# The first image pair of a 3x3 convolution loaded by eight DMAs of sixteen rows instead of one of 128

## The chip, the core and the metric

One core of a Trainium2 chip. The metric is the time of one execution on the device in microseconds (us). The kernel before takes 123.04 us (median of 3 runs, 122.94 to 123.07).

A core has engines with a program each: TensorE (PE in the profile, its weight loads PEld), VectorE (DVE), ScalarE (ACT), GpSimd (POOL) and SyncE (SP), which here only issues transfers. They meet by semaphores. Data moves between the device memory and SBUF (128 partitions, one row of a tile in each) by sixteen DMA engines, which all transfers share. A DMA adds 16 to its semaphore when it has landed.

## The reference

A 3x3 convolution with zero padding of 1 over 16 images of 64 channels and 64 x 64 pixels, 64 output channels, and the addition of a residual, all float32 at the border of the kernel:

```python
batch, c_in, h, w, c_out, k = 16, 64, 64, 64, 64, 3
x_pad = np.pad(x, ((0, 0), (0, 0), (pad, pad), (pad, pad)), mode='constant')
...
output[b, co] += weight[co, ci, kh, kw] * x_pad[b, ci, kh:kh+h, kw:kw+w]
...
return (output + residual).astype(np.float32)
```

x, residual and the output are 16.8 MB each.

## The kernel before

Images go in pairs: two images of 64 channels are 128 rows of 64 x 64 x 4 bytes = 16 KB, one row in each partition. `xr` holds three such pairs, `ro` the whole residual, which becomes the output in place.

```python
x_bc = x.rearrange("b c h w -> (b c) (h w)")
ro = pool.tile([128, NPAIR, NPIX], FP32)
xr = [nc.alloc_sbuf_tensor(f"xr{i}", [128, NPIX], FP32) for i in range(NXR)]   # NXR = 3
...
def load_x(p):
    return nc.sync.dma_start(out=xr[p % NXR][:, :], in_=x_bc[128 * p : 128 * p + 128, :]).then_inc(s_x[p % NXR], 16)
...
def store(pairs):
    return nc.sync.dma_start(out=out_bc[:, pairs, :], in_=ro[:, pairs, :])
```

All transfers are issued by SyncE, in this order. `to_the_front` takes the DMA just emitted and puts it into the program's first block, ahead of the barrier at which the engines meet when the program starts; so the first pair is asked for before anything else happens.

```python
for p in range(NPAIR):                                  # NPAIR = 8
    if p >= NXR:
        nc.sync.wait_ge(s_half, 2 * (p - NXR) + 3)      # ScalarE has read the buffer
    if p == 0:
        to_the_front(load_x(p))
        nc.sync.dma_start(out=wraw[:, :], in_=w_rows[:, :]).then_inc(s_w, 16)
    else:
        load_x(p)
    if p in (0, 1, 3, 5, 7):
        load_ro((p + 1) // 2)
for k in range(NEARLY):                                 # NEARLY = 3, two pairs each
    nc.sync.wait_ge(s_add, 4 * k + 5)
    store(slice(2 * k, 2 * k + 2)).then_inc(s_out, 16)
# ... and at the end of the program
for p in range(2 * NEARLY, NPAIR):
    store(slice(p, p + 1))
```

GpSimd makes the identity and the zero borders. TensorE transposes the weights (through `ps`), VectorE and ScalarE cast them into `wl`. Then for each image ScalarE casts the pair's rows to bfloat16 (`xp`), TensorE does 24 matmuls into one of two halves of PSUM, and VectorE adds the result to `ro`:

```python
for n in range(B):                                      # ScalarE, B = 16
    p, im = divmod(n, 2)
    ...
    if im == 0:
        nc.scalar.wait_ge(s_x[p % NXR], 16 * (p // NXR + 1))
    i = nc.scalar.copy(out=t[64:128, 0:J, :], in_=x4[hp, :, 0, :])
    i.then_inc(s_half, 1)
    ...
    nc.scalar.copy(out=t[0:64, 1 : J + 1, :], in_=x4[hp, :, 1, :]).then_inc(s_pack, 1)
```

Of the kernel before, what the change touches and what calls it, by code (L numbers as in the profile page):

```python
# [15 lines left out]
def kernel(  # L16
# [7 lines left out]
    nc = tc.nc  # L24
# [11 lines left out]
    NXR = 3  # L36
    NXP = 4
    NZERO = 4 + 2 * NXP
    NEARLY = 3
    RES = (slice(0, 1), slice(1, 2), slice(2, 4), slice(4, 6), slice(6, 8))  # L40

# [2 lines left out]
    x_bc = x.rearrange("b c h w -> (b c) (h w)")  # L44
# [7 lines left out]
    xr = [nc.alloc_sbuf_tensor(f"xr{i}", [128, NPIX], FP32) for i in range(NXR)]  # L52
# [8 lines left out]
    s_x = [sem(f"s_x{i}") for i in range(NXR)]  # L61
# [8 lines left out]

    def load_x(p):
        return nc.sync.dma_start(out=xr[p % NXR][:, :], in_=x_bc[128 * p : 128 * p + 128, :]).then_inc(s_x[p % NXR], 16)

    def load_ro(i):
        if i >= 2:
            nc.sync.wait_ge(s_r[i % 2], 16 * (i // 2))
        nc.sync.dma_start(out=ro[:, RES[i], :], in_=res_bc[:, RES[i], :]).then_inc(s_r[i % 2], 16)

    def store(pairs):
        return nc.sync.dma_start(out=out_bc[:, pairs, :], in_=ro[:, pairs, :])  # L80
# [21 lines left out]
    def to_the_front(dma):  # L102

        def fixed(ap):
            t = ap.bass_ap.tensor.name
            return mybir.PhysicalAccessPattern(
                ap=ap.ap, offset=ap.bass_ap.offset, dtype=ap.dtype, memref=t, memsetref=t + "_set", bass_ap=ap.bass_ap
            )  # L110

        front = nc.main_func.blocks[0].instructions
        here = nc.cur_bb.bb.instructions
        ins = here.pop()
        assert ins.name == dma.ins.name
        at = next(
            i for i, e in enumerate(front) if e.engine == ins.engine and isinstance(e, mybir.InstDrain)
        )
        front.insert(at, copy.replace(ins, ins=[fixed(a) for a in ins.ins], outs=[fixed(a) for a in ins.outs]))
# [5 lines left out]
    def weight_block(h, half, d, par, kh):  # L125

        at = 64 * half + 32 * h
        return dict(out=wl[at : at + 32, d, :, par, :], in_=tp[0:32, kh, 0:384].rearrange("p (kw co h) -> p kw co h", kw=3, h=2)[:, :, :, h])

    with tc.tile_critical(no_gpsimd_drain=True):  # L130

        for p in range(NPAIR):
            if p >= NXR:

                nc.sync.wait_ge(s_half, 2 * (p - NXR) + 3)
            if p == 0:
                to_the_front(load_x(p))
                nc.sync.dma_start(out=wraw[:, :], in_=w_rows[:, :]).then_inc(s_w, 16)
            else:
                load_x(p)  # L140
            if p in (0, 1, 3, 5, 7):
                load_ro((p + 1) // 2)
        for k in range(NEARLY):
            nc.sync.wait_ge(s_add, 4 * k + 5)
# [6 lines left out]
            out=ident[:, :],  # L151
            in_=ident[:, :],
# [14 lines left out]
        for n in range(B):  # L167
            p, im = divmod(n, 2)
            hp = slice(64 * im, 64 * im + 64)
            x4 = xr[p % NXR].rearrange("q (j two w) -> q j two w", two=2, w=W)  # L170
            t = xp[n % NXP]
            if im == 0:
                nc.scalar.wait_ge(s_x[p % NXR], 16 * (p // NXR + 1))
            i = nc.scalar.copy(out=t[64:128, 0:J, :], in_=x4[hp, :, 0, :])  # L174
            i.then_inc(s_half, 1)
            if n >= NXP:
                i._wait_ge(s_conv, n - NXP + 1)
            nc.scalar.copy(out=t[0:64, 1 : J + 1, :], in_=x4[hp, :, 1, :]).then_inc(s_pack, 1)  # L178
            if n == 0:
                nc.scalar.wait_ge(s_id, NZERO + 1)  # L180
                for b in blocks[4:]:
                    for h in range(2):
                        i = nc.scalar.copy(**weight_block(h, *b))  # L183
                i.then_inc(s_id, 1)


        nc.vector.wait_ge(s_id, NZERO + 1)
        for k, b in enumerate(blocks[:4]):
# [5 lines left out]
        for n in range(B):  # L194
            p, im = divmod(n, 2)
# [6 lines left out]
            for par in range(2):  # L202
                i = nc.vector.tensor_tensor(  # L203
                    out=o4[hp, :, par, :], in0=psj[64 * par : 64 * par + 64, :, :], in1=o4[hp, :, par, :], op=ADD
# [6 lines left out]

        nc.tensor.wait_ge(s_id, NZERO)
        nc.tensor.wait_ge(s_w, 16)
        wraw3 = wraw.rearrange("p (ci t) -> p ci t", t=9)
        for t in range(9):
            i = nc.tensor.transpose(  # L216
                out=tp[0:32, t // 3, 128 * (t % 3) : 128 * (t % 3) + 128], in_=wraw3[:, :, t], identity=ident[:, :]
            )
        i.then_inc(s_id, 1)
        nc.tensor.wait_ge(s_id, NZERO + 3)  # L220
        with nc.Fori(0, B // NXP, 1, engines=[PE]):
# [18 lines left out]

    for p in range(2 * NEARLY, NPAIR):
        store(slice(p, p + 1))
    with tc.tile_critical(sync_engine=mybir.EngineType.Pool, no_gpsimd_drain=True):
        nc.gpsimd.wait_ge(s_out, 16 * NEARLY)
        tc.free_semaphores([s_w, *s_x, *s_r, s_out, s_id, s_half, s_pack, s_bank, s_conv, s_add])
# [30 lines left out]
```

## Time and profile before

A profile is one execution taken by the hardware profiler; times in it are microseconds from the start of its span.

| | value |
|---|---|
| time, median of 3 | 123.04 us |
| span in the profile | 120.8 us |
| bytes moved | 50.48 MB: 33.70 read, 16.78 written |
| mean rate over the span | 418 GB/s |
| one image pair (2048 KB), median time from issue to landing | 15.3 us |
| ScalarE's first cast of the first pair starts | 7.79 us |
| first convolution matmul starts | 13.78 us |

How to read it: the page gives the busy share of each engine, a strip of forty slices of the span with a digit for tenths of busy time, the share of the DMA queue, the chain of work that ended last, and groups of instructions. Windows give the same for any stretch of the span, and the timeline lists instructions in order. The trace also has a record of each DMA packet (its start, its time and its bytes); a packet here is one row of 16 KB, or a row of the weights of 1152 bytes, or a completion write of 4 bytes at the end of a DMA on an engine. An engine that is idle costs nothing as long as it isn't the one that the others wait for.

### The profile page before, as it was taken

What the parts mean: (1) busy time and instruction counts of PE and PEld (TensorE: products, weight loads), DVE (VectorE), ACT (ScalarE), POOL (GpSimd) and SP (SyncE); (2) the same over time, 40 slices, a digit from 0 to 9 for tenths busy, and PEclk for the clock granted to TensorE, in tenths of its full rate; (3) what the DMA queues carried; (4) which work ended last, traced back from release to release, by engine and by line L of the source; (5) the groups of instructions that cost most, each with busy time, mean ns of one, the idle gap of its engine ahead of it and who ended that gap; (6) DMA issues with size and microseconds to landing.
All of it is one profiled execution on the core that took longest, in us unless ns stands there. A gap on an engine that the chain in (4) does not pass through costs nothing.

```text
span 120.8 us, 734 instructions
## 1 busy us (share of the span) xinstructions
PE 87.9 (73%) x393; PEld 10.7 (9%) x105; DVE 76.0 (63%) x40; ACT 63.1 (52%) x37; POOL 2.4 (2%) x16
## 2 busy tenths in 40 slices
PE   0024499999999999999999999999999990000000
PEld 0011001101010011011111111011111100000000
DVE  0005400789898988989879898988989879500000
ACT  4049959948999923999960999883000000000000
POOL 5200000000000000000000000000000000000000
PEclk9999999999999999999999999999999999855555
DMA  7999999999999999999999999999999999999994
GB/s 168 428 428 428 428 428 434 428 434 434 428 434 434 434 428 434 434 434 434 434 434 423 423 428 434 423 412 434 434 434 434 423 434 434 434 428 434 434 434 174
DMA packets 3504, 50.48 MB, mean 418 GB/s; under 512 B 304, under 2 KB 432, under 8 KB 432
## 3 DMA queue, kind: packets, MB, share of 16 engines
q1 hardware_dynamic: 3504, 50.48, 98.5%
HBM read 33.70 MB, written 16.78 MB: 418 GB/s over the span
## 4 chain that ended last, share of the span: by engine, by line
PE 71%; DVEq 2%; DVE 2%; issue 0%
PE ps L87 53%; PE ps L86 18%; DVEq L130 2%; DVE ro L203 2%
## 5 line engine op out<-in xcount | busy, mean ns | idle before, releaser
L203 DVE TENSOR_TENSOR ro<-ps,ro 64x2048 f32<-64x2048 f32 x32 | 73.2, 2289 | 17.7 <-PE ps L87 17.2
L87 PE MATMUL ps<-xp,wl 128*128 128x504 bf16 (+1 forms) x288 | 80.0, 388 | 0.0
L86 PE MATMUL ps<-xp,wl 128*128 128x504 bf16 (+1 forms) x96 | 37.4, 389 | 3.4 <-PEq L224 3.4
L174 ACT CAST xp<-xr 64x2048 bf16<-64x2048 f32 x16 | 30.3, 1896 | 18.3 <-DMA xr<-in_x_dram 17.2
L178 ACT CAST xp<-xr 64x2048 bf16<-64x2048 f32 x16 | 30.4, 1897 | 0.4
L86 PEld LDWEIGHTS ps<-xp,wl 128*128 128x128 bf16 x96 | 9.5, 99 | 79.1 <-issue 79.1
L190 DVE CAST wl<-ps 32x192 bf16<-32x192 f32 x8 | 2.8, 348 | 10.6 <-PE ps L216 10.5
L216 PE MATMUL ps<-ident,wraw 128*32 128x128 f32 x9 | 2.1, 413 | 8.3 <-DMA wraw<-in_weight_dram 8.3
L216 PEld LDWEIGHTS ps<-ident,wraw 128*32 128x32 f32 x9 | 1.2, 137 | 8.7 <-issue 8.2
L174 ACT ACT_TABLE_LOAD x1 | 1.3, 1283 | 1.0 <-SPq L130 1.0
L183 ACT CAST wl<-ps 32x192 bf16<-32x192 f32 x4 | 1.2, 306 | 0.0
L162 POOL MEMSET xp<- 64x64 bf16 x4 | 0.6, 147 | 0.2
L161 POOL MEMSET xp<- 64x64 bf16 x4 | 0.6, 145 | 0.2
L150 POOL TENSOR_SCALAR_AFFINE_SELECT ident<-ident 128x128 f32<-128x128 f32 x1 | 0.3, 294 | 0.2 <-POOL ident L148 0.2
L164 POOL MEMSET wl<- 64x192 bf16 x1 | 0.3, 253 | 0.1
L163 POOL MEMSET wl<- 64x192 bf16 x1 | 0.3, 252 | 0.1
L148 POOL MEMSET ident<- 128x128 f32 x1 | 0.2, 205 | 0.6 <-SPq L130 0.6
L260 POOL MEMSET const-bfloat16-1.0<- 128x1 bf16 x1 | 0.1, 112 | 0.0
L260 POOL MEMSET const-uint8-127<- 128x1 uint8 x1 | 0.1, 112 | 0.0
L260 POOL MEMSET const-float32-0.0<- 128x1 f32 x1 | 0.1, 105 | 0.2 <-issue 0.2
L260 POOL MEMSET const-float32-1.0<- 128x1 f32 x1 | 0.1, 109 | 0.0
## 6 DMA issues: line engine op xcount, KB each, us to landing
xr<-in_x_dram SPq DMA_DIRECT2D x8, 2048.0 KB, 15.3
ro<-in_residual_dram SPq DMA_DIRECT2D x3, 4096.0 KB, 24.0
out_dram<-ro SPq DMA_DIRECT2D x3, 4096.0 KB, 33.2
ro<-in_residual_dram SPq DMA_DIRECT2D x2, 2048.0 KB, 15.9
out_dram<-ro SPq DMA_DIRECT2D x2, 2048.0 KB, 12.8
wraw<-in_weight_dram SPq DMA_DIRECT2D x1, 144.0 KB, 7.1
```

The costliest lines, as they stand in the source:

```text
L86: return e.matmul(out=out_, lhsT=lhsT, rhs=rhs, start=start, stop=stop, skip_group_check=True)
L87: return e.add_instruction(mybir.InstMatmult(name=nc.get_next_instruction_name(), engine=PE, ins=[e.lower_ap(rhs), e.lower_ap(lhsT)], outs ...
L130: with tc.tile_critical(no_gpsimd_drain=True):
L161: nc.gpsimd.memset(t[0:64, 0, :], 0.0).then_inc(s_id, 1)
L162: nc.gpsimd.memset(t[64:128, J, :], 0.0).then_inc(s_id, 1)
L174: i = nc.scalar.copy(out=t[64:128, 0:J, :], in_=x4[hp, :, 0, :])
L178: nc.scalar.copy(out=t[0:64, 1 : J + 1, :], in_=x4[hp, :, 1, :]).then_inc(s_pack, 1)
L183: i = nc.scalar.copy(**weight_block(h, *b))
L190: i = nc.vector.tensor_copy(**weight_block(h, *b))
L203: i = nc.vector.tensor_tensor(out=o4[hp, :, par, :], in0=psj[64 * par : 64 * par + 64, :, :], in1=o4[hp, :, par, :], op=ADD)
L216: i = nc.tensor.transpose(out=tp[0:32, t // 3, 128 * (t % 3) : 128 * (t % 3) + 128], in_=wraw3[:, :, t], identity=ident[:, :])
L260: nc = _bacc.Bacc("TRN2", target_bir_lowering=False, num_devices=1)
```

## The change

The load of the first pair is cut into eight DMAs. DMA k takes the rows k, k + 8, ..., k + 120, so each has sixteen rows of 16 KB[...]. The first four go to the front of SyncE's program, ahead of the barrier; the other four follow behind it, ahead of the weights. ScalarE waits for all eight. The purpose is that all sixteen engines get work at once when the stream starts. No other engine's instructions change.

```diff
+    X0_FRONT = ((0, 1), (1, 1), (2, 1), (3, 1))
+    X0_BEHIND = ((4, 1), (5, 1), (6, 1), (7, 1))
...
+    def load_x0(k, n):
+
+        part = lambda t: t[k:128:8, :]
+        return nc.sync.dma_start(out=part(xr[0][:, :]), in_=part(x_bc[0:128, :])).then_inc(s_x[0], 16)
...
             if p == 0:
-                to_the_front(load_x(p))
+                for k, n in X0_FRONT:
+                    to_the_front(load_x0(k, n))
+                for k, n in X0_BEHIND:
+                    load_x0(k, n)
                 nc.sync.dma_start(out=wraw[:, :], in_=w_rows[:, :]).then_inc(s_w, 16)
...
-                nc.scalar.wait_ge(s_x[p % NXR], 16 * (p // NXR + 1))
+                nc.scalar.wait_ge(s_x[p % NXR], 16 * (p // NXR + (1 if p % NXR else len(X0_FRONT + X0_BEHIND))))
```

## The prediction

> **What bounds the kernel now.** I read the page first, its second and third parts before the engines.
>
> ```profile
> span 120.8 us, 734 instructions
> PE 87.9 (73%) x393; PEld 10.7 (9%) x105; DVE 76.0 (63%) x40; ACT 63.1 (52%) x37; POOL 2.4 (2%) x16
> ...
> DMA  7999999999999999999999999999999999999994
> ...
> q1 hardware_dynamic: 3504, 50.48, 98.5%
> ```
>
> No engine is above 73%, but the sixteen DMA engines together are busy 98.5% of the span, in every slice but the first and the last. The kernel is a stream of 50.48 MB with two ends: what happens before the first slice is full and after the last byte. The chain of waits names PE for 71% of the span; that chain ends at the last residual add, and the stream runs on behind it. The timeline of the last 24 us shows how far:
>
> ```profile
> 99.67 4.61 DVE L203 TENSOR_TENSOR ro<-ps,ro 64x2048 f32<-64x2048 f32 x2 [0.58 <-PE ps L87]
> 104.58 0.98 SPq L80 DMA_DIRECT2D out_dram<-ro  x2
> ```
>
> The last store is issued by 105.6 us, while packets go on until about 119.4. Its own 2 MB need 4.9 us, so they begin near 114.5: the compute has some 9 us of slack, and PE's chain is not what ends the kernel.
>
> Next the beginning, in windows (columns: stretch and its length, busy time of PE, PEld, DVE, ACT, POOL with instructions, clock, DMA share, GB/s; a packet's bytes are booked in the window in which it starts, so shares can exceed 1):
>
> ```profile
> 0.75:1.00 0.25, 0.00 (x0) 0.00 (x0) 0.00 (x0) 0.04 (x1) 0.00 (x1) 1.00 0.00 0
> 1.00:1.25 0.25, 0.00 (x0) 0.00 (x0) 0.00 (x0) 0.25 (x1) 0.20 (x1) 1.00 4.90 918
> 1.25:1.50 0.25, 0.00 (x0) 0.00 (x0) 0.00 (x0) 0.25 (x1) 0.07 (x1) 1.00 0.84 131
> 1.50:1.75 0.25, 0.00 (x0) 0.00 (x0) 0.00 (x0) 0.25 (x1) 0.23 (x1) 1.00 0.44 66
> 1.75:2.00 0.25, 0.00 (x0) 0.00 (x0) 0.00 (x0) 0.25 (x1) 0.16 (x2) 1.00 0.31 66
> 2.00:2.25 0.25, 0.00 (x0) 0.00 (x0) 0.00 (x0) 0.24 (x1) 0.20 (x2) 1.00 0.49 131
> ...
> 2.75:3.00 0.25, 0.00 (x0) 0.00 (x0) 0.00 (x0) 0.00 (x0) 0.16 (x2) 1.00 0.92 393
> ```
>
> 918 GB/s over 0.25 us is 14 packets of 16 KB: nearly all engines start their first row 1.0 to 1.25 us after the issue. Then hardly anything starts for 1.5 us, because those first packets are slow. The single packet records of the trace, joined end to start into sixteen chains, say it by engine: first packets take 0.72 to 2.03 us (on four engines the second is slow as well, 1.11 to 1.77); from about 3.1 us on every 16 KB packet starts 0.607 us after the one before, 27.0 GB/s an engine, to the end of the kernel, save for one small stall near 78 us. A completion write at the end of a DMA costs an engine 5 to 6 ns, a weight row 0.047 us. The eight rows of the first pair end at 6.44 to 7.42 us by engine.
>
> These close into a sum. The slowest engine ends the first pair at 7.42 us. Behind it stand 8 weight rows (0.38), 192 - 8 = 184 rows of 16 KB (111.7) and 18 completion writes (0.1): 119.6 us, and the last chain does end at 119.6. So whatever the slowest engine gains or loses in its first eight rows goes one for one to the end. Above the 120.8 us span lie 2.2 us of measured time, taken as unchanged.
>
> [...]
>
> **The change part by part.**
>
> Removed: one issue of 128 rows (0.38 us of SyncE's queue). Added: eight issues of sixteen rows. If each takes 0.33 to 0.57 us like the issues at the start of the timeline, the four at the front end at about 1.5 us instead of 0.38, and everything behind SyncE's barrier (GpSimd's constants, ScalarE's table load) comes 1.1 us later. GpSimd ended at 3.94 us and is needed at 8.2, the table load ended at 2.24 and is needed at 7.8: hidden. The issues of rows 4 to 7 come at about 2.1 to 3.6 us, the weights and the residual by about 4.5. An engine needs its fifth packet no earlier than 1.0 + 4 x 0.607 = 3.4 us and, with the slow first packets, nearer 5: no starving. Later waits of SyncE are for buffers that are freed by work on this same stream, and shift with it.
>
> Seven more completion writes on each engine: 7 x 5.5 ns = 0.04 us.
>
> The start: [...] First starts were spread from 1.01 to 1.28 us, so this is 0.2 us at best. The slow first packets aren't explained by it: the earliest starters are among those that lose most.
>
> [...] DMA k writes partitions k, k+8, ..., k+120. [...] 1.21 us a packet. Alone, that is 8 x 0.607 = 4.9 us more. But the slow start already keeps engines near half rate: the third packets start at 2.8 to 3.8 us, where two rows at half rate would end at 1.1 + 2 x 1.21 = 3.5. [...] 6 x 0.607 = 3.6 us. [...] With the completion writes: 3.6 - 0.3 + 0.04 = 3.4 us on the slowest engine, all of it on the path.
>
> Sum: 123.0 + 3.4 = 126.4 us, 2.7% slower, span about 124.2.
>
> **The rivals.** [...] Then only the small terms remain: +0.04 us, minus up to 0.2 for the start; 122.8 to 123.1, no visible change. [...] Second, the slow first packets come from the length of one big DMA and vanish: the slowest engine would end its rows at 1.0 + 8 x 0.607 = 5.9 instead of 7.4, worth 1.5 us, so 121.5. Against it: [...] no later DMA shows such first packets[...]. [...] Fourth, SyncE's issues starve the engines: nine issues ahead of the residual at 0.5 us are 4.5 us, under what the engines need for the data, so at most some tenths.
>
> **Range and chances.** [...] the vanished ramp 0.05. [...] even a perfect start (1.5 us, 1.2%) isn't 2% faster. So slower 0.66, same 0.33, faster 0.01. The range runs from 122.6 to 128.0 to hold both main outcomes.
>
> **What would show it right or wrong.** In the profile of the changed kernel: the packets of the first pair take about 1.2 us each until 10 to 11 us and the DMA rate in windows from 3 to 10 us is near 215 to 230 GB/s instead of 430, then 430 again to the end; the first cast of ScalarE starts near 11 us instead of 7.8, the first convolution matmul near 17 instead of 13.8; the span is about 124.2. [...] If 1 to 3 us is full as well, the slow start belonged to the big DMA. If the rate dips between 4 and 6 us with no packets pending, the issues were too slow. If the stream slows by 3 us early and the end moves less, the sum carried from the start to the end is wrong.

## The result, and the profile after

The changed kernel takes 127.13 us (127.10 to 127.14, 4 runs) beside 122.99 us for the kernel before on the same chip: ratio 1.0336, 95% interval 1.0319 to 1.0354. It is 4.1 us slower; 3.4 us were predicted.

The page of the changed kernel, its span, its engines, its DMA strip and its queue:

```profile
span 125.3 us, 737 instructions
...
PE 87.9 (70%) x389; PEld 10.7 (9%) x105; DVE 76.0 (61%) x40; ACT 63.1 (50%) x37; POOL 2.4 (2%) x16
...
DMA  7999999999999999999999999999999999999993
GB/s 178 209 209 262 434 429 424 418 434 439 439 429 429 424 418 434 439 445 429 424 424 429 439 434 439 429 424 418 429 445 450 424 424 424 424 439 439 439 429 167
...
q1 hardware_dynamic: 3616, 50.48, 98.3%
```

The engines' busy times and the bytes are what they were. The DMA strip shows the same nines as before, so the busy share says nothing here; the GB/s line below it tells the story: in the second to fourth slices (3 to 12.5 us) the DMA engines are "busy" and move about half as much, and from the fifth on the rate is that of before. The same line of the kernel before:

```profile
GB/s 168 428 428 428 428 428 434 428 434 434 428 434 434 434 428 434 434 434 434 434 434 423 423 428 434 423 412 434 434 434 434 423 434 434 434 428 434 434 434 174
```

The 112 additional packets are seven more completion writes on sixteen engines (packets under 512 B: 304 before, 416 after).

Windows of the changed kernel (columns as in the prediction: stretch and length, busy time by engine, clock, DMA share, GB/s):

```profile
1.00:2.00 1.00, 0.00 (x0) 0.00 (x0) 0.00 (x0) 0.00 (x0) 0.00 (x0) 1.00 0.94 262
2.00:3.00 1.00, 0.00 (x0) 0.00 (x0) 0.00 (x0) 0.00 (x0) 0.00 (x0) 1.00 1.14 262
3.00:7.00 4.00, 0.00 (x0) 0.00 (x0) 0.00 (x0) 1.28 (x1) 2.17 (x12) 1.00 0.97 209
7.00:10.00 3.00, 0.00 (x0) 0.00 (x0) 0.00 (x0) 0.00 (x0) 0.00 (x0) 1.00 1.14 235
14.00:18.00 4.00, 0.72 (x4) 0.17 (x2) 2.78 (x8) 3.92 (x7) 0.00 (x0) 1.00 1.01 434
```

The same three later stretches of the kernel before:

```profile
3.00:7.00 4.00, 0.00 (x0) 0.00 (x0) 0.00 (x0) 0.00 (x0) 0.78 (x4) 1.00 0.96 409
7.00:10.00 3.00, 1.73 (x9) 1.16 (x9) 0.00 (x0) 2.18 (x2) 0.00 (x0) 1.00 1.09 460
14.00:18.00 4.00, 4.00 (x10) 0.30 (x2) 0.00 (x0) 2.70 (x3) 0.00 (x0) 1.00 1.01 434
```

From 3 to 7 us 209 instead of 409 GB/s at the same share. Half the rate at full occupation means packets that take twice as long (1.24 us instead of 0.611 in the table below), not engines that wait for work. The first cast and the first convolution matmul follow the data, in the timeline of the changed kernel:

```profile
0.00 5.74 SPq L79 DMA_DIRECT2D xr<-in_x_dram  x8
...
12.29 1.90 ACT L184 CAST xp<-xr 64x2048 bf16<-64x2048 f32 x1 [7.72 <-DMA xr<-in_x_dram]
...
18.16 0.58 PE L93 MATMUL ps<-xp,wl 128*128 128x512 bf16 x1 [3.44 <-PEq L234]
```

Before they started at 7.79 and 13.78 us, so both are 4.4 to 4.5 us later. The prediction named about 11 and 17 us and a span of 124.2 us; all three came 1.1 to 1.3 us later than that. Of the 4.5 us, 4.03 are the rows themselves (table below); from the last row's end to the cast pass 0.84 us instead of 0.37. Why isn't shown; the compute has slack for it. By the first line SyncE is through with the eight issues at 5.74 us: 4.6 us of issues and 0.9 us at the barrier between the fourth and the fifth.

The packet records, read by engine as in the prediction, in numbers (us from the start of the span; "middle rows" are the 33rd to 112th of the first pair's 128 rows in order of start):

```
                                       before    after
first packet starts                      1.01     1.37
median of the first 16 rows              1.55     1.00
median of the middle rows                0.611    1.24
last row of the first pair ends          7.42    11.45
last weight row ends                     7.80    12.04
last packet ends                       119.62   123.96
```

The shift at the end of the weights is 12.04 - 7.80 = 4.24 us, at the last packet 4.34 us, in the measured time 4.14 us. What was lost in the first 12 us came to the end one for one, within 0.1 us.

### The profile page after: what moved, and what is told of

It is laid out like the page before. It is cut to its first block, busy times and chain, and to the rows that moved or that the text cites. A ratio compares the mean times of both kernels' runs of the same rounds, so it can differ in the third digit from the quotient of the medians.

```text
span 125.3 us, 737 instructions
## 1 busy us (share of the span) xinstructions
PE 87.9 (70%) x389; PEld 10.7 (9%) x105; DVE 76.0 (61%) x40; ACT 63.1 (50%) x37; POOL 2.4 (2%) x16
## 3 DMA queue, kind: packets, MB, share of 16 engines
q1 hardware_dynamic: 3616, 50.48, 98.3%
## 4 chain that ended last, share of the span: by engine, by line
PE 69%; DVEq 2%; DVE 2%; issue 0%
PE ps L94 52%; PE ps L93 17%; DVEq L137 2%; DVE ro L213 2%
## 5 line engine op out<-in xcount | busy, mean ns | idle before, releaser
L94 PE MATMUL ps<-xp,wl 128*128 128x504 bf16 (+1 forms) x288 | 80.2, 388 | 0.2
L93 PE MATMUL ps<-xp,wl 128*128 128x504 bf16 (+1 forms) x92 | 35.9, 390 | 3.4 <-PEq L234 3.4
```

The lines of the kernel that those rows point to most:

```text
L93: return e.matmul(out=out_, lhsT=lhsT, rhs=rhs, start=start, stop=stop, skip_group_check=True)
L94: return e.add_instruction(mybir.InstMatmult(name=nc.get_next_instruction_name(), engine=PE, ins=[e.lower_ap(rhs), e.lower_ap(lhsT)], outs ...
```

## The experiments

The theory on trial: the rows take 1.24 instead of 0.611 us because of the SBUF partitions that each of the eight DMAs covers. Rivals: the rows are read at a 128 KB step in memory and that is slow; short DMAs are slow by their number, their issue or their completions. Every time stands beside the kernel before on the same chip. The first four ran together: 122.84 us for before.

**Adjacent rows in memory, the same SBUF partitions.** This mixes up the rows of the first pair, so its two images come out as other sums; the work is the same.

```diff
-        ... dma_start(out=part(xr[0][:, :]), in_=part(x_bc[0:128, :]))
+        ... dma_start(out=part(xr[0][:, :]), in_=x_bc[16 * k : 16 * k + 16, :])
```

> Eight DMAs of sixteen rows as in the changed kernel, SBUF partitions still k, k+8, ..., but read from sixteen adjacent rows of device memory (the rows of the first pair are permuted, so its two images are not the reference's). Theory [...]: nothing changes, packets stay at 1.1 to 1.26 us, time 127.0 +- 0.4. Rival (the 128 KB step between the rows read is what is slow): packets fall to 0.61 us, time 123.0 to 124.0, the rest being the slow issues.

Measured: 126.92 us, ratio 1.0328 (1.0311 to 1.0346), middle rows 1.26 us. Windows of this kernel:

```profile
7.00:8.00 1.00, 0.00 (x0) 0.00 (x0) 0.00 (x0) 0.00 (x0) 0.00 (x0) 1.00 1.18 246
8.00:9.00 1.00, 0.00 (x0) 0.00 (x0) 0.00 (x0) 0.00 (x0) 0.00 (x0) 1.00 0.96 197
```

Still half the rate, and 4.08 us lost; the step in memory is not the cause.

**Adjacent rows in memory and in SBUF.**

```diff
-        part = lambda t: t[k:128:8, :]
+        part = lambda t: t[16 * k : 16 * k + 16, :]
```

> Eight DMAs of sixteen adjacent rows, adjacent in memory and in SBUF: [...] packets of 2.43 us, eight of them 19.4 us instead of 4.9, the first pair lands near 20.5 to 21, time 123.0 + 13 to 14.5 = 136 to 137.5. Rival (step of the memory rows): 123 to 124. Rival (slow because of short DMAs as such, with their issue of 0.6 us and their completion): 127, as changed.

Measured: 135.01 us, ratio 1.0992 (1.0973 to 1.1010), middle rows 2.22 us. Windows of this kernel:

```profile
7.00:10.00 3.00, 0.00 (x0) 0.00 (x0) 0.00 (x0) 0.00 (x0) 0.00 (x0) 1.00 1.13 131
14.00:18.00 4.00, 0.00 (x0) 0.00 (x0) 0.00 (x0) 0.00 (x0) 0.00 (x0) 1.00 0.65 75
```

131 GB/s, and 75, where the kernel before shows 460 and 434 in the same stretches (in the second stretch packets of 2.2 us are booked by their starts, so a window can catch too few). The rows are now as contiguous as they can be, the DMAs as many as in the changed kernel, the bytes the same, and three times as much is lost: 12.2 us against 4.1. Memory rows and number of DMAs are those of the run before it; only the SBUF partitions differ, and rows go from 1.26 to 2.22 us. So neither the memory step nor the number of short DMAs explains it; the set of partitions does. Per row: 0.611 us in one DMA of all 128 partitions, 1.24 in sixteen partitions in steps of 8 (1.26 with adjacent memory rows), 2.22 in sixteen adjacent ones. The records show times and sizes; how a set of partitions comes to its rate isn't shown. The time was one microsecond better than expected: 2.43 us a row was my estimate, 4 x 0.607, with no run behind the factor of four, and the first row of each engine takes only 1.31 us in the median. Sixteen rows of 16 KB in 2.22 us are 118 GB/s.

**Eight DMAs of an eighth of the columns, all 128 rows.** The split, the placing and the number stay; every DMA covers all 128 partitions again.

```diff
-        part = lambda t: t[k:128:8, :]
+        part = lambda t: t[:, 512 * k : 512 * k + 512]
```

> Eight DMAs again, four in front and four behind, same semaphore counts, but each takes an eighth of the columns (2 KB) of all 128 rows[...]. [...] the data runs at 430 GB/s as far as the issues allow; the first pair lands at 7.0 to 8.0 us, time 122.8 to 123.6. Rival (eight DMAs cost it by their number: issues, completions): 126 to 127.

Measured: 124.60 us, ratio 1.0138 (1.0121 to 1.0154). More than half of the loss is gone, but 1.8 us stay, which I had not expected. Windows of this kernel:

```profile
3.00:4.00 1.00, 0.00 (x0) 0.00 (x0) 0.00 (x0) 0.66 (x1) 0.72 (x5) 1.00 1.00 358
4.00:5.00 1.00, 0.00 (x0) 0.00 (x0) 0.00 (x0) 0.00 (x0) 0.78 (x5) 1.00 0.84 283
5.00:6.00 1.00, 0.00 (x0) 0.00 (x0) 0.00 (x0) 0.00 (x0) 0.30 (x2) 1.00 0.72 229
```

The median packet of 2 KB takes 0.084 us (24 GB/s an engine), so an engine's 64 packets need 5.4 us where eight rows of 16 KB need 4.9, and single ones take up to 1.1 us. Besides, engines stand idle here: 0.8 us each in the mean from their first packets to 12 us, most of it from 4 to 7 us, against 0.01 us in the changed kernel. Whether the slower packets come from the shorter rows or from the number of DMAs this run doesn't separate.

**Four DMAs of 32 rows in steps of 4, two in front.**

```diff
-    X0_FRONT = ((0, 1), (1, 1), (2, 1), (3, 1))
-    X0_BEHIND = ((4, 1), (5, 1), (6, 1), (7, 1))
+    X0_FRONT = ((0, 1), (1, 1))
+    X0_BEHIND = ((2, 1), (3, 1))
...
-        part = lambda t: t[k:128:8, :]
+        part = lambda t: t[k:128:4, :]
```

> Four DMAs of 32 rows in steps of 4 partitions, two in front, two behind. [...] Open is which rows an engine gets: if two neighbouring rows (8e+k and 8e+4+k), [...] packets of 1.2 us, time 126 to 127. [...] packets are 0.61 us and the time is 122.5 to 123.2. [...] the rival of slow short DMAs expects about half of the loss, 125.

Measured: 123.72 us, ratio 1.0063 (1.0044 to 1.0082), middle rows 0.62 us. Most rows of 16 KB in steps of four partitions take what they took before (0.611 us): the step isn't slow as such. Of the two packet times expected, 1.2 and 0.61 us, it is the lower; which rows an engine gets isn't shown. The remaining 0.9 us isn't a doubling of all rows: first packets start at 1.32 us instead of 1.01, and of the 41 rows that start between 4.05 and 5.95 us, about when the two DMAs behind the barrier are under way, about half take 0.7 to 2.0 us. Why isn't shown.

The next four ran beside 122.95 us for before.

**The changed kernel with the weights behind the first residual.**

```diff
                 for k, n in X0_BEHIND:
                     load_x0(k, n)
-                nc.sync.dma_start(out=wraw[:, :], in_=w_rows[:, :]).then_inc(s_w, 16)
...
                 load_ro((p + 1) // 2)
+            if p == 0:
+                nc.sync.dma_start(out=wraw[:, :], in_=w_rows[:, :]).then_inc(s_w, 16)
```

> The changed kernel with the weights' load moved behind the first residual. In the changed kernel the eight weight rows of an engine took 0.10 us each instead of 0.05, which adds 0.4 to 0.5 us to the slowest engine. [...] the rows take 0.05 us here and the time is 126.6 to 126.8; [...] first pair's data ends near 11.2 us. Rival (sixteen engines meeting in the weights' 147 KB at the same time): rows stay at 0.10 us, time 127.1.

Measured: 127.36 us, ratio 1.0356 (1.0339 to 1.0373). The weight rows are at 0.051 us again, as the first expectation had it, and yet nothing was gained. First pair, weights and first residual are through at 16.92 us in both kernels: here the residual takes 16.54 - 11.45 = 5.09 us instead of 8 x 0.607 = 4.86. So it isn't a cost of the weights; here the residual, which comes behind the first pair, pays it. And the compute, which now starts another 4.9 us later, has used up its slack of 9 us (4.3 + 4.9 = 9.2). Windows of this kernel, and the same stretch of the changed kernel behind it:

```profile
110.00:118.00 8.00, 0.00 (x0) 0.00 (x0) 3.46 (x2) 0.00 (x0) 0.00 (x0) 0.74 0.93 395
```

```profile
110.00:118.00 8.00, 0.00 (x0) 0.00 (x0) 0.00 (x0) 0.00 (x0) 0.00 (x0) 0.50 1.00 428
```

VectorE is still adding at 110 us (its last add ends at 113.5) and the stream waits for the last stores: 395 GB/s, and each DMA engine stands idle for about 0.6 us near 114 us. Here the compute, led by PE, takes part in setting the end.

**The kernel before, with the later issues held back.**

```diff
                 to_the_front(load_x(p))
+                nc.sync.wait_ge(s_id, NZERO - 2)
```

> The kernel before, with SyncE waiting for GpSimd's zero borders (about 3.5 us) before it issues anything behind the first pair. Theory A: the first packets of 0.7 to 2.0 us are slow because five more DMAs are being issued at the same time; then they fall to 0.61 us, the first pair's data ends at 6.0 to 6.3 us and the time is 121.8 to 122.2. Theory B: they are slow as the first packets of the program whoever else is issuing: nothing changes, 122.7 to 123.1.

Measured: 122.93 us, ratio 0.9999 (0.9988 to 1.0011). The next issue is at 3.35 us and the first sixteen rows still take 1.45 us in the median. The slow start isn't made by the issues behind it.

**The first pair in two DMAs, a narrow one ahead.**

```diff
-    X0_FRONT = ((0, 1), (1, 1), (2, 1), (3, 1))
-    X0_BEHIND = ((4, 1), (5, 1), (6, 1), (7, 1))
+    X0_FRONT = ((0, 288), (288, 4096))
+    X0_BEHIND = ()
...
-        part = lambda t: t[k:128:8, :]
+        part = lambda t: t[:, k:n]
```

> The first pair as two DMAs of all 128 rows, both in front: the first 288 columns (1152 bytes a row), then the remaining 3808. Theory B (the path is slow for whoever comes first): the small rows take the slow start, the large ones run at 0.57 us from about 2.5 us on; since the small rows hold up each engine for 1 to 2 us all the same, time 122.6 to 123.4. If the slowness is one of large first packets, the small rows take 0.05 us, the large ones are slow: 122.9 to 123.4, told apart by the packets and not by the time.

Measured: 122.94 us, ratio 1.0003 (0.9992 to 1.0013). Most narrow rows take 0.05 us from the first on (some 0.2 to 0.35); the wide rows that follow from 1.5 us on take 0.9 to 1.5 us until about 3 us, and 0.58 us then. So neither theory's picture fits whole: the first packet is not slow because it is first, but about 2 us of traffic run at some 250 GB/s (here 266 and 186 from 1 to 3 us, 295 and 213 in the kernel before), in narrow rows and in wide ones.

**Two DMAs of 64 rows in steps of 2, both in front.**

```diff
-    X0_FRONT = ((0, 1), (1, 1), (2, 1), (3, 1))
-    X0_BEHIND = ((4, 1), (5, 1), (6, 1), (7, 1))
+    X0_FRONT = ((0, 1), (1, 1))
+    X0_BEHIND = ()
...
-        part = lambda t: t[k:128:8, :]
+        part = lambda t: t[k:128:2, :]
```

> Two DMAs of 64 rows in steps of 2 partitions, both in front of the barrier[...]. [...] packets of 0.61 us, no gap in front of the barrier: time 122.8 to 123.3, as before the change. If part of the loss with 32 rows (0.9 us) was not the barrier but the number of DMAs: 123.3 to 123.7.

Measured: 123.28 us, ratio 1.0042 (1.0026 to 1.0059), middle rows 0.611 us; the weights are through at 8.01 us, 0.2 us after those of before. A window of this kernel:

```profile
3.00:7.00 4.00, 0.00 (x0) 0.00 (x0) 0.00 (x0) 0.29 (x1) 1.53 (x9) 1.00 0.95 400
```

400 GB/s, where the kernel before has 409 and the changed one 209. A cut in two, both in front, runs at the rate of before and gains nothing over one DMA.

The last two ran beside 122.86 us for before.

**Sixteen rows in steps of 7.**

```diff
-        part = lambda t: t[k:128:8, :]
+        part = lambda t: t[k : k + 106 : 7, :] if k < 7 else t[112:128, :]
```

> The changed kernel with another choice of sixteen rows: DMA k takes partitions k, k+7, ..., k+105 for k from 0 to 6, [...] the last DMA takes partitions 112 to 127 [...]. Rows, bytes, issues and completions stay as in the changed kernel. [...] in the first seven DMAs most packets behind the slow start take 0.61 us; the last DMA's packets take about 2.2 us and start near 6 to 7 us; the first pair lands near 9 us, time 124.3 to 125.3. Rival (sixteen-row DMAs in steps of partitions are slow as such): packets of 1.2 us throughout, time 127 or more.

Measured: 126.65 us, ratio 1.0297 (1.0267 to 1.0328): outside both expectations. Windows of this kernel:

```profile
4.00:5.00 1.00, 0.00 (x0) 0.00 (x0) 0.00 (x0) 0.59 (x1) 0.72 (x6) 1.00 0.96 295
5.00:6.00 1.00, 0.00 (x0) 0.00 (x0) 0.00 (x0) 0.00 (x0) 0.76 (x5) 1.00 0.96 279
6.00:7.00 1.00, 0.00 (x0) 0.00 (x0) 0.00 (x0) 0.00 (x0) 0.25 (x1) 1.00 1.11 328
7.00:8.00 1.00, 0.00 (x0) 0.00 (x0) 0.00 (x0) 0.00 (x0) 0.00 (x0) 1.00 1.12 262
...
9.00:10.00 1.00, 0.00 (x0) 0.00 (x0) 0.00 (x0) 0.00 (x0) 0.00 (x0) 1.00 0.75 81
```

280 to 330 GB/s from 4 to 7 us is between the changed kernel's 180 to 230 and the 409 of before from 3 to 7 us, with middle rows of 0.92 us. The last DMA's sixteen rows start only at 7.8 to 9.3 us and take 1.39 us in the median (at most 1.99), not 2.2. I had estimated a rate for each DMA by itself, and engines are not in step (their first rows start at 1.37 to 1.95 us), so rows of two DMAs may be under way at once; whether that sets the rate isn't shown. This run the estimates got wrong, and its cause stays open. Part of the 0.92 us may belong to DMAs of sixteen rows as such. Sixteen rows in steps of four partitions, the step that took 0.62 us a row in DMAs of 32, could tell that apart; no run tried it.

**The kernel before, its first pair behind the barrier.**

```diff
-                to_the_front(load_x(p))
+                load_x(p)
```

> The kernel before with the first pair's one DMA behind the barrier instead of in front. Theory B1 (the slow start belongs to the first two microseconds of traffic): all is later by the barrier, about 0.9 to 1.0 us, with the same slow first packets: 123.8 to 124.1. Theory B2 (it belongs to the time since the program's start, up to 3 us): first packets start near 2 us and are nearly over it, the slowest engine loses only some tenths: 122.9 to 123.4.

Measured: 123.70 us, ratio 1.0073 (1.0047 to 1.0098). First packets start at 1.99 us, 0.98 later, and the first sixteen rows still take 1.28 us in the median. The slow start goes with the traffic and not with the program's clock, as the first theory had it, at 0.1 us below its range; the place in front is worth 0.84 us.

Shifts against before, at the end of the weights in the profile and in the measured time (us):

```
                                     weights   time
adjacent in memory, steps of 8         3.97    4.08
adjacent, steps of 1                  11.81   12.17
columns                                2.12    1.76
32 rows, steps of 4                    1.04    0.88
64 rows, steps of 2, in front          0.21    0.33
steps of 7                             3.93    3.79
not in front                           0.82    0.84
```

Seven kernels, and the delay of the first microseconds is the delay of the end within 0.4 us each time. (The profile of the kernel with held-back issues shows 0.45 us at the weights and its median time none; its profiled execution took 123.37 us, 0.44 above that median.)

## Why the prediction was right

The direction and the size class held; 127.13 us lies 0.7 us above the point. The half rate on which the sum was built, 1.21 us a row, was an estimate of mine, twice the 0.607 of before, for which no trace of before gave a ground. It is in the trace now (209 of 409 GB/s); why this set of partitions halves the rate isn't shown. That the time lies in the range says little, since the range of 122.6 to 128.0 was to hold "no change" as well.

1. The stream as the bound, and the carry to the end: right, by the table above. The slack of 9 us for compute is right too: the run with the later weights used 9.2 us of it, and then the DMA engines stood idle for about 0.6 us.
2. The half rate: right. The windows from 3 to 10 us were predicted at 215 to 230 GB/s and show 209 and 235. Giving each of the eight DMAs all 128 partitions (columns) loses 1.76 instead of 4.14 us. If the cut as such costs the changed kernel no more than that, its choice of partitions accounts for at least 2.4 us; this condition isn't shown. Sixteen adjacent partitions in place of steps of 8, with nothing else changed, triple the loss (12.17 instead of 4.08 us). What no estimate foretold is the run with steps of 7.
3. How the slower rows lie over the slow start: right in the sum, with luck in its parts. From its first packet to the last row, the first pair takes 11.45 - 1.37 = 10.08 us instead of 7.42 - 1.01 = 6.41, that is 3.67 us more; the prediction's six rows at 0.607 and its completion writes were 3.64 + 0.04 = 3.68. But the rows in order of start, sixteen at a time, take (medians) 1.55, 0.61, 0.63 and then 0.61 us before, and 1.00, 1.19, 1.23, 1.25, 1.11, 1.24, 1.26, 1.26 after. So seven rows pay about 0.6 us each and not six, and the first gives 0.55 back. A loss of all eight rows, the 4.9 us, is out: the first rows don't get slower, but faster.
4. The 0.3 us taken off in the sum: about half of it is there. The fifth sixteen rows in order of start take 1.11 us instead of 1.24, and in the mean of the engines the eight rows take 9.45 us instead of 5.91, 3.54 more and not 3.68. The 0.3 was an estimate without a measurement behind it.
5. The start: wrong in sign. Up to 0.2 us of gain was named; the first packet starts 0.36 us later. This goes with the issue of DMAs whose SBUF rows are stepped. Issues of the first pair in the changed kernel, then in the kernel with adjacent rows (minimum, median, maximum ns):

```profile
L79 SPq DMA_DIRECT2D xr<-in_x_dram x8: 492/586/594, 0.0 to 5.1; - x8
```

```profile
L79 SPq DMA_DIRECT2D xr<-in_x_dram x8: 310/412/420, 0.0 to 3.7; - x8
```

   With steps in SBUF an issue takes 0.59 us, without them 0.41, and the first packet starts at 1.36 us with adjacent memory rows but SBUF steps, at 1.06 us without either. I had taken 0.33 to 0.57 from the issues of before; so the four in front end at 2.5 us and not at 1.5, and everything behind the barrier comes 2.3 us later and not 1.1. That was hidden, as predicted.
6. Not in the sum: the delay outlasts the first pair. The last weight row ends 0.58 us after the first pair instead of 0.38, 0.2 us more, and where the weights come later the residual pays it.

3.67 + 0.36 + 0.20 = 4.23 us, the shift at the end of the weights to rounding. What was mis-sized is the deduction (0.3, of which about 0.14 came), the start (0.36 later, where up to 0.2 earlier was named) and the tail (0.2, left out).

The rival of the vanished slow start is out: two or eight DMAs, held-back issues and a narrow head leave about 2 us of traffic at some 250 GB/s (from 1 to 3 us 213 and 279 with two DMAs, 262 and 262 with eight, 262 and 279 with held-back issues, 266 and 186 with the narrow head). The rival of starving issues did not act in the changed kernel: its engines go from packet to packet, idle for 0.01 us in the mean from their first packets to 12 us. It did act in the columns, with 0.8 us. The columns, with all 128 partitions in each DMA, and the 32 rows, at 0.62 us a row, kept 1.8 and 0.9 us, so cutting the first load had a price of its own in both; in the changed kernel the slower rows may cover it. What else it consists of stays open: issues behind the barrier, shorter rows and the number of DMAs were not separated.

## What to carry to other kernels

Look at which SBUF partitions each DMA covers: with sixteen partitions in steps of 8 the first pair ran at half rate with a DMA share near 1 (209 instead of 409 GB/s here), with sixteen adjacent ones at 131 GB/s. These runs don't show how to foretell the rate of another set, so measure it. Read GB/s beside the busy share, and packet times beside both. In a kernel that is one saturated stream, as this one (DMA queue 98.3% of the span), the first load is on the path to the last microsecond (seven delays came to the end within 0.4 us), so leave it as one DMA over all 128 partitions unless a run shows a faster shape; none of the cuts tried here was faster.

## What was not expected of the hardware

- Sixteen adjacent partitions to a DMA: 2.22 us a row, where I had estimated 2.43; sixteen in steps of 8: 1.24 us; one DMA of all 128: 0.607 us from start to start.
- DMAs of 32 and 64 rows in steps of 4 and 2 partitions run at the rate of one DMA (0.62 and 0.611 us a row, 0.611 before), and no set of sixteen partitions tried here does (0.92, 1.24 and 2.22 us).
- The first 2 us of traffic run at about 250 GB/s, whether they start at 1.0 us (295 and 213 GB/s from 1 to 3 us) or at 2.0 us (229 and 279 from 2 to 4 us), with the later issues held back (262 and 279), or with narrow rows ahead (266 and 186). No run here shortened it, and its cause is open.
- A DMA issue with SBUF partitions in steps of 8 takes SyncE 0.59 us in the median (0.56 in steps of 4 and of 2), one with adjacent partitions 0.41 us. An adjacent one right behind stepped ones can take as long: 0.58 us for the weights in the changed kernel.
